# The down projection of a hybrid encoder block as seven part products over 2x2 blocks, in one stream with up

## The chip, the cores and the metric

The kernel runs on one core of a Trainium2 chip. The metric is the device time of one execution in microseconds, the median of several runs. A core has TensorE (PE in the profile: matmuls; PEld: its weight loads), VectorE (DVE), ScalarE (ACT), GpSimd (POOL) and SyncE (SP, which here issues all DMAs). All operands lie in SBUF, products in PSUM, which has eight banks of 128 partitions x 512 f32.

## What is computed

One layer of an encoder over x of 2048 tokens x 1024 channels, in f32: an input projection, an mLSTM head group and a latent attention group side by side, an output projection, a gated MLP with a centred convolution of three taps, and a gated per-layer embedding. What matters here is the MLP and what follows it:

```python
def conv_gated_mlp(xn, w_up, conv_w, conv_b, w_down):
    u = dwconv3_centred(xn @ w_up, conv_w, conv_b)
    gate, val = jnp.split(u, 2, axis=-1)
    return (jax.nn.silu(gate) * val) @ w_down
...
h = h + conv_gated_mlp(rms_norm(h, ln_ffn_g[l]), w_up[l], conv_ffn_w[l], conv_ffn_b[l], w_down[l])
gate = jax.nn.sigmoid(rms_norm(h, ple_norm_g[l]) @ w_ple_gate[l])
h = h + gate * rms_norm(p[l] @ w_ple_proj[l], ple_post_g[l])
return rms_norm(h, final_g)
```

w_up is 1024 x 5632 (gate and value halves of 2816), w_down is 2816 x 1024: 22 channel tiles of 128 on the side that down sums over.

## The kernel before

**Arithmetic.** Each f32 operand is split into a high part (rounded to the matmul's f32 format, by ACT) and a low part (the difference, by DVE): `split`, L112 to L119. A product of two split operands is three matmuls (`mm3`, L127: low x high, high x low, high x high), which accumulate into one PSUM bank. A matmul here has a stationary operand of 128 x 128 and a moving one of 128 x 512.

**Order.** The code is written with tile pools. A tile is taken by its tag (`at`, L103; tags x.., w.., t.., u..), and a tag is a place in SBUF: a new tile of a tag waits for the last reader of the old one. The scheduler of the framework orders the instructions of each engine's queue and each DMA when the kernel is built. It goes mainly by the order in which they are written, but takes later ones first where an earlier one would wait; at run time each queue is strictly in order. PSUM is four tiles of two banks (`two`, L167), from two pools by turns.

**Up (`up`, L1288).** 44 pairs: two passes over the tokens (tokens 0 to 1023, then 1024 to 2047), each over 22 channel tiles c. One pair computes the gate and the value columns of channel tile c for the pass's 1024 tokens. As a 2x2 by 2x2 block product it has the stationary blocks A11, A12 (gate columns, lower and upper half of the 1024 input channels) and A21, A22 (value columns), and the moving blocks B11, B12, B21, B22 (input channel halves x token halves of 512). Instead of eight block products, seven are made, with sums of blocks: A11·B11, S1·T1, S2·T2, A12·B21, S3·T3, A22·T4, S4·B22. Each is four channel tiles x three matmuls (`prod`, L1297). The seven need three banks x, y, z in which products of several outputs accumulate one after another, with evictions in between: x holds A11·B11 and then A12·B21 too, y holds S2·T2, then S3·T3, then A22·T4 too, z holds S1·T1 and later S4·B22 too. The last two products of a pair (`rest`, L1308) stand inside the next pair. A matmul that adds to a bank waits until the eviction that reads it is done: S3 waits for the add at L1385 that reads S2 out of y. x goes out through ACT (L1363, L1395), the rest through DVE.

The moving operands of a pass, split, lie in the x places (`OPX`, seven names). They are loaded from DRAM by `load_op` (L1207) through raw buffers t0 to t5, 28 pieces of 128 x 512 for a pass; T1 to T4 were formed by `sums` (L1174) and stored in `t_d`, for the second pass during pairs 6, 9, 12 and 15 of the first. At the last pair of the first pass, each name is replaced as soon as its last product is written (`last`, L1366 to L1410); T4 and B22 follow in the next pair.

The stationary operands of pair i+1 are split and summed by `up_prep` (L1256) within pair i, and the raw weights of pair i+2 are fetched by `up_load` (L1221). In the first pass the sums S are formed and kept in `s_d`; the second pass loads them.

`conv` (L1315) takes the finished gate and value columns of the previous pair, applies the three taps, SiLU and the product, and writes the hidden tile to `hid_d` in DRAM. It uses the places w7 and w11, and u0, u1, u2 for its inputs. After the last pair a short computation forms the hidden value of the last token (L1417 to L1425).

**Down (`down`, L1441).** Four blocks of 512 tokens. For each, eight PSUM banks (`facc`: four token tiles x 1024 output columns) accumulate over all 22 channel tiles: per channel tile, 4 token tiles x 2 halves x 3 matmuls. The hidden tile is the stationary operand (loaded and split once per block by `load_hid`, L1446), the rows of w_down are the moving one (loaded and split again in every block by `load_w`, L1432). At the end of a block the residual (`h1_d`) is added to `facc` (L1489) and the result is stored in `h2_d`.

**The last stage (`ple`, L1495)** is a generator. It is started at down's last block and advanced there at channel tiles 11 to 20 (L1476), which loads and splits the two tiles of w_ple_proj and the eight of w_ple_gate under the block's matmuls. The rest runs after down, over 16 token tiles: normalise, transpose, project, gate, final norm.

Of the kernel before, what the change touches and what calls it, by code (L numbers as in the profile page):

```python
# [19 lines left out]
P = 128  # L20
S = 2048
# [39 lines left out]
class Block:  # L61
# [4 lines left out]
    def __init__(self, ctx, tc, d):  # L66
# [30 lines left out]
        self.t_d = dt([2, 4, P, 4, 512], F32, name="t_d")  # L97
        self.s_d = dt([NC2, 2, P, D], F32, name="s_d")
# [47 lines left out]
    def run(self, out):  # L146
# [15 lines left out]
        self.up()  # L162
        self.down(out)
# [1006 lines left out]

    OPX = {"B11": (8, 9), "T1": (12, 13), "T2": (14, 15), "B21": (0, 1), "T3": (2, 3), "T4": (4, 5), "B22": (6, 7)}
    PAIRS = (("w3", "w4"), ("x10",), ("w5", "w6"), ("x11",), ("w8", "w9"))

    def sums(self, b):  # L1174


        nc = self.nc
        t0 = b * 2 * SB
        if not b:
            self.xop = {n: self.op_places(n) for n in ("B11", "T1", "T2")}  # L1180
        for k in range(4):
            r = []
            for i in range(4):
                kt, o = k + i // 2 * 4, t0 + i % 2 * SB
                r.append(self.at(f"t{i}", [P, SB], name="tsum"))
                nc.sync.dma_start(r[i], self.x2_d[:, kt, o:o + SB])
            b11, b12, b21, b22 = r
            tt = nc.vector.tensor_tensor
            put = lambda n, t: self.split(t, self.xop[n][0][:, k], self.xop[n][1][:, k])
            if not b:  # L1190
                put("B11", b11)
            tt(b12, b12, b11, op=ALU.subtract)
            tt(b22, b22, b12, op=ALU.subtract)
            tt(b11, b22, b11, op=ALU.subtract)
            tt(b21, b21, b22, op=ALU.subtract)
            if not b:
                put("T1", b12)
                put("T2", b22)
            for i, t in enumerate((b12, b22, b11, b21)):
                if b or i > 1:  # L1200
                    nc.sync.dma_start(self.t_d[b, i, :, k], t)
            yield

    def op_places(self, n):
        return [self.at(f"x{x}", [P, 4, SB], F32R, f"op{e}") for x, e in zip(self.OPX[n], "hl")]

    def load_op(self, b, n):  # L1207

        hi, lo = self.xop[n] = self.op_places(n)
        for k in range(4):  # L1210
            raw = self.at(next(self.orot), [P, SB], name="opr")
            if n[0] == "T":
                src = self.t_d[b, int(n[1]) - 1, :, k]
            else:
                o = b * 2 * SB + (int(n[2]) - 1) * SB
                src = self.x2_d[:, (int(n[1]) - 1) * 4 + k, o:o + SB]
            self.nc.sync.dma_start(raw, src)
            self.split(raw, hi[:, k], lo[:, k])
            yield

    def up_load(self, i):  # L1221


        nc = self.nc
        b, c = divmod(i, NC2)
# [18 lines left out]

    def up_pair(self, src):
        self.npair = getattr(self, "npair", -1) + 1
        tags = self.PAIRS[self.npair % 5]
        if len(tags) == 1:
            t = self.at(tags[0], [P, 2, D], F32R, "fw2")
            hi, lo = t[:, 0], t[:, 1]  # L1250
        else:
            hi, lo = [self.at(t, [P, D], F32R, "fw1") for t in tags]
        self.split(src, hi, lo)
        return [(hi[:, o:o + SB], lo[:, o:o + SB]) for o in (0, SB)]

    def up_prep(self, i):  # L1256

        nc = self.nc
        b, c = divmod(i, NC2)
# [5 lines left out]
        a22 = flat(raw[1]) if b else flat(raw[1])[:, SB:]  # L1265
        d = self.at(("w2", "w10")[i % 2], [P, 2, SB], F32R, "fwd")
# [4 lines left out]
        else:  # L1271
            sv, sg = flat(raw[1]), g
            lo, hi = slice(0, SB), slice(SB, D)
# [3 lines left out]
        ops["S3"], ops["S1"] = self.up_pair(sv)  # L1277
        if not b:
            nc.sync.dma_start(self.s_d[c, 0], sv)
# [353 lines left out]
```

## Time and profile before

| | us |
|---|---|
| median of three runs (lowest, highest) | 3025.64 (3020.70, 3027.59) |
| the profiled execution's own time | 3022.41 |
| its span, first to last instruction | 3020.6 |
| up: 1438 to 2280 in that span | 842 |
| down: 2280 to 2780 | 500 |
| last stage: 2780 to the end | 240 |

The granted clock of the profiled execution is 0.997 of full speed, on its one core.

How to read a profile's rows here: a group has the line, engine, operation, the tile written and the tiles read, the shape and the count, then the total busy time and the mean of one in ns, then the idle time of that engine ahead of these instructions with what ended it. A window row has a stretch of the span and each engine's busy time within it. A timeline row has the start and the length, both in us. A wait row has who waited for whom, and then the total, the times and the longest. Since the split and the matmul are helpers, L119, L116 and L129 stand for many places; the names of tiles tell them apart: `facc` is down, `fxy` and `fzs` are up's banks (x with y, z with a spare), `fw`, `fws` and `fwd` are weights, `oph` and `opl` moving operands.

### The profile page before, as it was taken

How to read it: one execution, taken by the hardware profiler on the slowest of the kernel's cores; microseconds unless marked ns; L12 is line 12 of the kernel's file. 1: busy time of each engine (PE TensorE's matmuls, PEld its weight loads, DVE VectorE, ACT ScalarE, POOL GpSimd, SP SyncE). 2: the span in 40 equal slices, each digit the busy share in tenths (PEclk: the TensorE clock that was granted, in tenths of full speed). 3: DMA queues.
4: the chain of work that ended last, by engine and by line, in shares of the span. 5: the costliest groups of instructions: out<-in, count | busy, mean ns of one | idle time of the engine just before them, and what ended most of it. 6: DMA issues, size and time to landing. Idle time of an engine off the chain costs nothing. (4 is left out here: it accounts for less than half of the span.)

```text
span 3020.6 us, 40579 instructions
## 1 busy us (share of the span) xinstructions
PE 2966.4 (98%) x15122; PEld 2505.6 (83%) x15122; DVE 1892.7 (63%) x3441; ACT 1355.2 (45%) x2598; POOL 141.5 (5%) x262
## 2 busy tenths in 40 slices
PE   8999999999999999999999999999999999999998
PEld 7888887889888888888778877888887888878887
DVE  7421556767767777646888889777776333334665
ACT  7211545556565566423444446444445232223444
POOL 3100000000000000001000000000000000000111
PEclk9999999999999999999999999999999999999999
DMA  6522445343323333668654445334337465444221
GB/s 191 110 76 91 139 126 167 111 138 118 95 93 97 95 125 114 192 209 268 229 188 139 140 139 197 126 124 126 126 122 251 167 209 202 133 153 148 79 79 63
DMA packets 322917, 430.03 MB, mean 142 GB/s; under 512 B 24976, under 2 KB 218528, under 8 KB 322720
## 3 DMA queue, kind: packets, MB, share of 16 engines
q1 hardware_dynamic: 322720, 427.44, 44.0%
q8 instruction: 119, 1.95, 0.3%
q14 instruction: 78, 0.64, 0.1%
HBM read 292.17 MB, written 135.20 MB: 141 GB/s over the span
## 5 line engine op out<-in xcount | busy, mean ns | idle before, releaser
L129 PE MATMUL facc<-fw,hid 128*128 128x512 f32 x2112 | 482.0, 390 | 6.2 <-DVE ug L1313 2.7
L129 PEld LDWEIGHTS facc<-fw,hid 128*128 128x128 f32 x2112 | 397.2, 188 | 90.1 <-DVE ug L1313 3.1
L129 PE MATMUL fxy<-oph,fw 128*128 128x512 f32 x1408 | 449.5, 392 | 6.0 <-DVE ug L1385 5.0
L129 PEld LDWEIGHTS fxy<-oph,fw 128*128 128x128 f32 x1408 | 264.2, 188 | 75.1 <-DVE ug L1385 11.5
L119 DVE TENSOR_TENSOR fw<-fwr,fw 128x1024 fp32r<-128x1024 f32 x176 | 215.1, 1223 | 163.0 <-ACT fw L116 162.9
L116 ACT CAST fw<-fwr 128x1024 fp32r<-128x1024 f32 x176 | 184.9, 1051 | 258.7 <-PE facc L129 123.2
L129 PE MATMUL fxy<-opl,fw 128*128 128x512 f32 x704 | 274.8, 390 | 0.0
L129 PE MATMUL bk<-wsp,xh 128*128 128x512 f32 (+1 forms) x768 | 234.4, 386 | 1.5 <-DVE wsp L125 1.4
L129 PE MATMUL fzs<-oph,fw 128*128 128x512 f32 x704 | 234.3, 389 | 1.2 <-DVE xt L1134 1.2
L116 ACT CAST pt<-tb 128x512 fp32r<-128x512 f32 x256 | 146.8, 586 | 192.8 <-PE tb L959 192.5
L129 PE MATMUL ppv<-pt,kv 128*128 128x256 f32 x1536 | 203.3, 287 | 0.0
L901 DVE TENSOR_REDUCE mx<-bk 128x1 f32<-128x512 f32 x256 | 174.7, 684 | 44.9 <-PE bk L900 43.6
L119 DVE TENSOR_TENSOR pt<-tb,pt 128x512 fp32r<-128x512 f32 x256 | 173.9, 685 | 35.8 <-ACT pt L116 34.1
L129 PEld LDWEIGHTS ppv<-pt,kv 128*128 128x128 f32 x1536 | 188.8, 191 | 0.0
L919 ACT ACTIVATE pe<-bk,nm 128x512 f32<-128x512 f32 x256 | 174.2, 694 | 25.5 <-DVE nm L913 24.4
L129 PE MATMUL pgp<-pw,x3s 128*128 128x512 f32 (+1 forms) x792 | 178.7, 385 | 0.0
L129 PE MATMUL bk<-wo,yhl 128*128 128x512 f32 x744 | 175.4, 392 | 0.0
L129 PEld LDWEIGHTS pgp<-pw,x3s 128*128 128x128 f32 x792 | 144.4, 188 | 28.3
L129 PEld LDWEIGHTS bk<-wsp,xh 128*128 128x128 f32 x768 | 144.2, 189 | 28.3 <-DVE wsp L125 3.5
L129 PEld LDWEIGHTS bk<-wo,yhl 128*128 128x128 f32 x744 | 138.2, 188 | 28.1
L129 PE MATMUL bk<-wsp,xl 128*128 128x512 f32 (+1 forms) x384 | 150.5, 392 | 9.6 <-ACT wsp L124 8.5
L129 PE MATMUL bk<-xh,wqk 128*128 128x512 f32 x480 | 156.8, 393 | 0.0
(322 smaller groups left out, 5352.4 us busy)
## 6 DMA issues: line engine op xcount, KB each, us to landing
fwr<-in_w_down SPq DMA_DIRECT2D x88, 512.0 KB, 3.8
fwr<-in_w_up SPq DMA_DIRECT2D x66, 512.0 KB, 4.1
s_d<-fwr SPq DMA_DIRECT2D x44, 512.0 KB, 3.2
fws<-s_d SPq DMA_DIRECT2D x44, 512.0 KB, 3.6
hraw<-hid_d SPq DMA_DIRECT2D x33, 512.0 KB, 4.2
rw<-row_d SPq DMA_DIRECT2D x32, 512.0 KB, 4.9
hid_d<-fgv SPq DMA_DIRECT2D x22, 512.0 KB, 3.5
hid_d<-fgv SPq DMA_DIRECT2D x22, 511.5 KB, 5.1
```

The source lines that it names most:

```text
L116: nc.scalar.copy(hi, src)
L119: (sub or nc.vector).tensor_tensor(lo, src, _f(hi), op=ALU.subtract)
L129: mm = lambda *a, **k: self.nc.tensor.matmul(*a, **k, skip_group_check=more)
L901: nc.vector.tensor_reduce(s.mx[:, kb:kb + 1], ps, axis=AX.X, op=ALU.max)
L919: nc.scalar.activation(s.pe[:, kb % 2], s.banks[kb], AF.Exp, bias=s.nm, scale=ASCALE, accum_out=s.rs[:, kb:kb + 1])
```

## The change

`up` and `down` become one method, `up_down`, with one list of five blocks of pairs: the two passes of up as before, and three parts of down. A part of down covers 8, 8 and 6 of the 22 channel tiles that down sums over. Each part has eight pairs, one for every two token tiles. In a down pair the stationary blocks are hidden rows (token tile x half of the part's channel tiles) and the moving blocks are parts of w_down (half of the channel tiles x 512 output columns): two halves of 4, 4 or 3 channel tiles. The seven products run as in up, with 12 matmuls each (9 in the third part).

The two output tiles of a pair are loaded into `fh` tiles (`down_out`: `h1_d` in the first part, `h2_d` after it), every product's bank is added into them by DVE, and they are stored to `h2_d`: outputs go through DRAM three times. The five places for them (`hrot`) are u0, w7, w11, u1, u2. For the first down pair the load stands behind the last `conv`; from then on it stands one pair ahead.

The stationary operands come from `down_load` (two tiles of 128 tokens from `hid_d`) and `up_prep`, which forms the sums as in the first pass of up but keeps none. The moving sums T1 to T4 of w_down are formed by `wsums` and kept in `tw_d`: the first part's during four pairs of up's second pass, the others' during the part before. `load_op` replaces the operands at the last pair of each block, as it did between the passes. The x places are cut anew: a place holds two channel tiles, each with its high and low part, and in the third part neighbouring names share places, so that x1, x5 and x13 become free.

```diff
-        self.up()
-        self.down(out)
+        self.up_down(out)
...
+    OPX3 = {"B11": (8, 8, 9), "T1": (9, 12, 12), "T2": (14, 14, 15), "B21": (15, 0, 0), "T3": (2, 2, 3), "T4": (3, 4, 4),
+            "B22": (6, 6, 7)}
+    NUP = 2 * NC2
+    BLOCKS = ((0, NC2, 4), (NC2, NC2, 4), (2 * NC2, 8, 4), (2 * NC2 + 8, 8, 4), (2 * NC2 + 16, 8, 3))
...
+    def wsums(self, g):
+        kk = self.BLOCKS[2 + g][2]
+        for k in range(kk):
+            self.sum4(lambda i: self.w_down(g, k, i), lambda i: self.tw_d[g, i, :, k], {})
+            yield
...
+    def sum4(self, src, dst, ops):
...
+        for i in range(4):
+            r.append(self.at(f"t{i}", [P, SB], name="tsum"))
+            nc.sync.dma_start(r[i], src(i))
+        b11, b12, b21, b22 = r
...
+        tt(b12, b12, b11, op=ALU.subtract)
+        tt(b22, b22, b12, op=ALU.subtract)
+        tt(b11, b22, b11, op=ALU.subtract)
+        tt(b21, b21, b22, op=ALU.subtract)
...
+        for i, t in enumerate((b12, b22, b11, b21)):
+            if not ops or i > 1:
+                nc.sync.dma_start(dst(i), t)
...
+    def down_load(self, i):
+        nc = self.nc
+        g, pr = divmod(i - self.NUP, 8)
+        n = 2 * self.BLOCKS[2 + g][2]
+        tags = ("w12", "w13", "w0", "w1")[i % 2 * 2:i % 2 * 2 + 2]
...
+            nc.sync.dma_start(t[:, :, :m], self.hid_d[8 * g:8 * g + n, :, o:o + m].rearrange("c p t -> p c t"))
...
+    def down_out(self, i):
+        g, pr = divmod(i - self.NUP, 8)
+        out = []
+        for e in range(2):
+            t = self.at(next(self.hrot), [P, D], name="fh")
+            self.nc.sync.dma_start(t, (self.h2_d if g else self.h1_d)[2 * pr + e])
+            out.append(t)
+        return out
...
         def rest(s):
             prod(s.y, s.ops["A22"], "T4", True)
-            tt(s.uv[:, 2:2 + SB], s.p1, s.y, op=ALU.add)
+            if s.down:
+                add(s.o[1][:, L], s.o[1][:, L], s.y)
+                nc.sync.dma_start(self.h2_d[2 * s.pr + 1], s.o[1])
+            else:
+                add(s.uv[:, 2:2 + SB], s.p1, s.y)
             prod(s.z, s.ops["S4"], "B22", True)
...
+                add(s.o[0][:, H], s.o[0][:, H], s.z)
+                nc.sync.dma_start(self.h2_d[2 * s.pr], s.o[0])
...
+        self.hrot = _rot("", ("u0", "w7", "w11", "u1", "u2"))
...
             prod(x, s.ops["A11"], "B11")
...
+            if s.down and s.o:
+                add(s.o[0][:, H], s.o[0][:, H], x)
+                o2 = s.o[1].rearrange("p (a t) -> p a t", a=2)
+                add(o2, o2, x.unsqueeze(1).broadcast_to([P, 2, SB]))
...
             if prev:
                 rest(prev)
+                if prev.i == NUP - 1:
+                    conv(prev)
+                    s.o = self.down_out(i)
+                    add(s.o[0][:, H], s.o[0][:, H], x)
...
             prod(s.y, s.ops["S2"], "T2")
+            if s.down:
+                add(s.o[0][:, H], s.o[0][:, H], s.y)
...
             prod(x, s.ops["A12"], "B21", True)
+            if s.down:
+                add(s.o[0][:, L], s.o[0][:, L], x)
...
+            if s.down and i + 1 < n:
+                outs[i + 1] = self.down_out(i + 1)
...
             prod(s.y, s.ops["S3"], "T3", True)
+            if s.down:
+                add(s.o[1][:, H], s.o[1][:, H], s.y)
+                add(s.o[1][:, H], s.o[1][:, H], s.z)
```

`ple` is advanced within the last part (`side`): the two projection weights, the first gate weight and the norm gain at its pairs 2, 3 and 4, the loading and the norm of token tile 0 at pair 5, the transposes of that tile into the spare bank of z at pairs 6 and 7, gate weights 1 to 6 within pair 7 as each of the operands' places comes free, and gate weight 7 and the first projection ahead of the last `rest`. The gain is applied in two halves, since it now lies in t4 and t5. Its other tiles have other places; the loop over the token tiles stays.

## The prediction

> **What bounds the kernel now.** I read the page's busy times first, then windows of the two stages that change, then the rows of the pair of products that the change reuses.
>
> ```profile
> span 3020.6 us, 40579 instructions
> ...
> PE 2966.4 (98%) x15122; PEld 2505.6 (83%) x15122; DVE 1892.7 (63%) x3441; ACT 1355.2 (45%) x2598; POOL 141.5 (5%) x262
> ...
> 1438.00:2280.00 842.00, 833.28 (x3648) 1.00 0.46 151
> 2280.00:2780.00 500.00, 493.79 (x2172) 1.00 0.54 182
> 2780.00:3020.00 240.00, 232.94 (x1104) 0.99 0.22 76
> ...
> L129 PE MATMUL facc<-fw,hid 128*128 128x512 f32 x2112 | 482.0, 390 | 6.2 <-DVE ug L1313 2.7
> ...
> 2523.64 36.66 PE L129 MATMUL facc<-fw,hid 128*128 128x512 f32 x161
> ```
>
> The last three columns of a window are granted clock, DMA share, GB/s. PE is idle for 8.7 us of up (1438 to 2280), 6.2 of down (2280 to 2780) and 7.1 of the last stage: everywhere the number of matmuls sets the time. Matmuls overlap, so the 390 ns of one is not its price; 161 of them in a row take 36.66 us, of which the last shows 0.39, so one costs 36.27 / 160 = 0.2267 us. Down's 2112 are 478.8 us.
>
> Up is already made of seven part products, so its pairs show what a down pair will look like.
>
> ```profile
> 2243.10 0.68 DVE L1385 TENSOR_TENSOR ug<-p,fxy 128x512 f32<-128x512 f32 x1
> ...
> 2262.17 0.68 DVE L1385 TENSOR_TENSOR ug<-p,fxy 128x512 f32<-128x512 f32 x1
> ...
> 1460.00:1850.00 390.00, 385.22 (x1680) 1.00 0.47 158
> ...
> 1489.00:1508.00 19.00, 18.37 (x81) 14.77 (x80) 17.38 (x24) 8.47 (x11) 0.00 (x0) 1.00 0.73 247
> 1603.00:1622.00 19.00, 19.00 (x85) 15.43 (x84) 15.57 (x21) 8.47 (x11) 0.00 (x0) 1.00 0.40 139
> 1850.00:1869.00 19.00, 18.71 (x82) 15.03 (x81) 17.93 (x26) 14.70 (x24) 0.00 (x0) 1.00 0.92 290
> 1869.00:1888.00 19.00, 18.08 (x78) 14.18 (x77) 18.59 (x26) 13.21 (x22) 0.00 (x0) 1.00 0.71 235
> 1888.00:1907.00 19.00, 17.82 (x79) 14.27 (x78) 16.61 (x25) 8.14 (x11) 0.00 (x0) 1.00 0.40 134
> 1926.00:1945.00 19.00, 19.00 (x85) 15.67 (x84) 13.73 (x16) 8.46 (x11) 0.00 (x0) 1.00 0.37 124
> ```
>
> One pair of up is 84 matmuls and lasts 19.07 us. After the window's length the columns are PE, PEld, DVE, ACT, POOL busy, then clock and DMA. The first of these 19 us windows is a first-pass pair that also runs a step of `sums` (DVE 17.4), the second a plain first-pass pair (15.6), the next three the change of pass, the last a plain second-pass pair (13.7). PE loses nothing in plain pairs; it loses when DVE is near full.
>
> **What is removed.** Down needs 7 products x (4+4+3) channel tiles x 3 matmuls x 8 token pairs = 1848 matmuls instead of 2112: 264 fewer, at 0.2267 us a gain of **59.8 us**, all on PE, the bounding engine. The old down's own idle, **6.2 us**, goes too. The two waits behind most of it (facc behind L1313, and behind weight splits) are re-priced below.
>
> **What a down pair adds to DVE and ACT.**
>
> ```profile
> L119 DVE TENSOR_TENSOR fw<-fwr,fw 128x1024 fp32r<-128x1024 f32 x176 | 215.1, 1223 | 163.0 <-ACT fw L116 162.9
> L119 DVE TENSOR_TENSOR fwd<-fwr,fwd 128x512 fp32r<-128x512 f32 x44 | 30.4, 692 | 0.1
> L1275 DVE TENSOR_TENSOR fwr<-fwr 128x512 f32<-128x512 f32 x22 | 15.2, 691 | 0.7
> L1489 DVE TENSOR_TENSOR fh<-fh,facc 128x1024 f32<-128x1024 f32 x16 | 19.0, 1218 | 7.3 <-PE facc L129 6.5
> L119 DVE TENSOR_TENSOR opl<-opr,oph 128x512 fp32r<-128x512 f32 x44 | 28.4, 686 | 3.6 <-ACT oph L116 2.8 <-PE bk L129 0.7
> ```
>
> `up_prep` of a down pair is three 1024-wide splits, one of 512 and four sums: 3 x 1.223 + 0.692 + 4 x 0.691 = 7.1 us. The outputs are seven 512-wide adds (0.69, as the sums) and the broadcast add of x into both halves (1024 wide, 1.218 as L1489): 6.0 us. Together 13.1 us beside 19.04 us of PE. In the third part 512 wide costs 0.69 and 1024 wide 1.22, so 768 is 0.96 and 384 is 0.56: 5.7 + 6.0 = 11.7 us beside 63 matmuls, 14.28 us. That is 69% and 82% of the pair; 13.73 and 15.57 of 19 (72% and 82%) ran without loss above. ACT does 3.8 us of casts and stays far from bounding. Steady cost: the rows run from nothing (the 1926 window) to (390 - 385.22) = 4.8 us over 20.5 pairs, 0.23 each, with steps of `sums` and none. I take the latter, since `wsums` runs in seven of the 24 pairs and weight splits of the last stage in others: 24 x 0.23 = **5.6**, bounds 0 and 18. The upper bound comes from this wait:
>
> ```profile
> who waited for it (us, times):
>   PEld fxy L129: 11.5, 22
>   PE fxy L129: 5.0, 6
> ```
>
> These are the matmuls that waited for the eviction at L1385, that is for S3 to go into the bank that S2 left. The two rows partly count the same gaps; added, they are 16.5 / 22 = 0.75 us where it happened, and x, which ACT evicts in up (L1363, L1395), is then DVE's too: 24 x 0.75 = 18.
>
> The first `wsums` puts four steps of 4 x 0.69 = 2.7 us into second-pass pairs: 13.7 + 2.7 = 16.4 of 19, less than the 17.4 above, which lost 0.63. I take **1 us**, bounds 0 and 2.5.
>
> **The change from up to down (pairs 43 and 44)** is the dear place. Twenty operand splits of 0.686 (13.7 us) land in pair 43, eight (5.5) in 44, as at the change of pass. There DVE's work is 15.6 + 13.7 + 13.7 + 5.5 = 48.5 us, less the 5.5 of T4 and B22, which have another pair's time: 43.0 over two pairs of 19.07, 4.9 too much, and the three windows lost 0.29 + 0.92 + 1.18 = 2.4 us. Here pair 43 has 13.7 + (7.1 - 4.4 of a second-pass prep) + 13.7 = 30.1, and pair 44 has 13.1, plus the last `conv`, which without a next pair's conv to hide among comes on top:
>
> ```profile
> 2295.28 0.39 PE L129 MATMUL fzs<-oph,fw 128*128 128x512 f32 x1
> ...
> 2303.31 0.19 DVE L1420 TENSOR_TENSOR elast<-edge,fcw 128x44 f32<-128x44 f32 x1
> 2303.43 1.28 DVE L1327 SCALAR_TENSOR_TENSOR fgv<-ug,fcw,fgv 128x1024 f32<-128x1024 f32 x1
> ...
> 2306.00 1.23 DVE L1333 TENSOR_TENSOR fgv<-fgv 128x1024 f32<-128x1024 f32 x1
> ...
> fh<-h_d SPq DMA_DIRECT2D x16, 512.0 KB, 6.0
> ```
>
> 4 x 1.28 + 1.23 + five short edge terms like L1420's, 1.0, is 7.4: 26.0 with its 5.5 of splits, 20.5 without; 50.6 over 38.1, 12.5 too much. By the ratio of the pass change the first half of its 4.9 is absorbed, so 12.5 - 2.5 = **10 us** is lost. A second way agrees roughly. Pair 44's outputs are loaded only behind that conv (`down_out(44)` needs w7, the buffer of the last conv), so x cannot leave its bank until then: last product of pair 43 to the end of L1333 took 11.6 us here (2295.67 to 2307.23), the load 6.0, the adds 0.7 + 1.2: 19.5 us in which PE has S2 and S3 of 44 and A11, S1, S2 of 45, five products of 12 x 0.2267 = 13.6 us: 6 short. PE does take such work from ahead of the program's order (facc matmuls stand among the last up pair's). On SP, behind the waiting load, stand pair 46's hidden rows and the loads of T4 and B22; on DVE, behind x's add, y's and the splits of 45. Bounds: 2.4, and 19.5 if nothing fills it.
>
> **The changes between the parts (51/52, 59/60)** have no conv: DVE 13.1 + 13.7 + 13.1 = 39.9 over 38.1, below the pass change. DMA is what could bind. A pair moves 2 x 512 KB each of hidden rows, old outputs and new outputs (3.1 MB), and the operands 28 x 256 KB (7.3 MB): 13.6 MB in 38 us. The best 19 us row is 290 GB/s, at which this takes 47 us, 9 too long. SP's issues are no bound:
>
> ```profile
> L1217 SPq DMA_DIRECT2D opr<-t_d x24: 319/323/994, 1371.2 to 1871.8; - x24
> ```
>
> 6 in a plain pair and 20 more at a change are 26 x 0.32 = 8.3 of 19 us. T4 and B22 may slip a pair, and the 139 GB/s of plain pairs leaves room. I take 3 each, **6 us**, bounds 1 and 18 for both. The Trainium skill ("DMA: Bandwidth & Descriptors", Specifications) gives 435 GB/s as the fabric's ceiling. By that rule the 13.6 MB take 31 us and these 6 us vanish (2975); the row at share 0.92 stays a third below it, so I keep the row.
>
> **The end.** Gate weights 1 to 7 move from the old block 3 into the last pair and behind it.
>
> ```profile
> pwr<-in_w_ple_gate SPq DMA_DIRECT2D x8, 512.0 KB, 4.3
> ...
> L116 ACT CAST pw<-pwr x10: 1048/1052/1055, 2710.3 to 2770.3; 128x1024 fp32r<-128x1024 f32 x10
> L119 DVE TENSOR_TENSOR pw<-pwr,pw x10: 1218/1225/1227, 2711.5 to 2771.6; 128x1024 fp32r<-128x1024 f32 x10
> ```
>
> Two raw buffers turn round in 4.3 + 1.05 + 1.22 = 6.6 us, 3.3 a weight. Two are there when S1 of the last pair frees their places, some 4 us into it; the seventh is split 1.2 + 2.5 x 6.6 later, near 22 to 23 us. PE has the pair (14.3), `rest` (4.1), the first projection (2.7) and the gate's products with the first seven weights (21 x 0.2267 = 4.8): 26 us of cover. I take **2**, bounds 0 and 8 (if that cover is gone, one turn of a buffer and more). The transposes and projection of token tile 0 only move; the last stage is otherwise the same.
>
> **The sum.** The profiled execution took 3022.41 us, 1.8 more than its span of 3020.6; the median of the runs shown is 3025.64, 3.2 above it, so against that the same saving would read 2984. 3022.4 - 59.8 - 6.2 + 5.6 + 1 + 10 + 6 + 2 = **2981.0 us**.
>
> The longest wait of PE in these stages is
>
> ```profile
> PEld facc L129 <- DVE ug L1313: 3.1, 1, 3.1
> ```
>
> and the granted clock stays at 1.00 in every window of them. The Trainium skill ("TensorE: Matmul & The Clock Gate", Part 1) says that PE falls to half its clock after an idle window of about 3.4 us, which speaks against a stall such as the one at pair 44. By that rule the matmuls of one such window take twice as long, an estimate of 2 to 3 us more (2984); no row here shows it.
>
> **Rivals.** (a) All cover works: only the pass-change price at 43/44 and the steady idle remain: 3022.4 - 66.0 + 2.4 + 5.6 = 2964. For it: no loss in 1603 to 1622 at DVE 82%. Against it: each of three changes brings more than the pass change did. Chance 0.14. (b) DMA binds at the part changes and in the four pairs with `wsums` (3.1 + 2.1 MB in 19 us, 275 GB/s): 18 instead of 6 at the changes and 1 in each of those pairs: 2997. For it: share 0.92 at 1850; against it: the operands can be fetched early. Chance 0.12. (c) Slower: the y bank becomes a round trip. In each down pair S3 waits for DVE to evict S2, and the next pair's `rest` for it to evict S3, with DVE deep in `up_prep`; in the third part only 2.04 us of A12 lie between. The longest single waits were
>
> ```profile
> PE fxy L129 <- DVE ug L1385: 5.0, 6, 1.7
> ...
> PEld fxy L129 <- DVE ug L1385: 11.5, 22, 2.1
> PEld fxy L129 <- DVE uv L1404: 1.9, 2, 1.6
> ```
>
> (total, times, longest). If every pair paid both, 2.1 + 1.6 = 3.7, it is 24 x 3.7 = 88.8: 3022.4 - 66.0 + 88.8 + 19 = 3064. It decides from (66.0 - 19) / 24 = 1.96 us a pair, four times today's mean wait. DVE then would be at some 80% of the stage, and it ran at 94% (17.93 of 19) with almost no loss; hence 0.12. (d) That there is no saving in matmuls can't be: the loop counts give 1848. The forecast has the remaining 0.62, with a range of its own from 2968 (no steady idle, the pass-change price at 43/44) to 2993 (0.75 us in every pair).
>
> **How the numbers follow.** Some 6 us, 0.2%, is about what a measurement tells from no change. Forecast, (a) and (b) are all faster, 0.88; I move 0.04 of it to "same", for several terms at their upper ends together. Faster 0.84, same 0.04, slower 0.12. The range 2960 to 3008 leaves out most of (c) and a little at the bottom.
>
> **What would show it.** Right: 264 matmuls fewer; the down pairs 19.0 us apart in two parts and 14.3 in the third; about 10 us of PE idle around the last conv, behind DVE adds into `fh`; DVE over 85% busy in down. Wrong: idle of PE above 1 us in plain down pairs, or clock below 1.00 there; idle at the part changes with the DMA share below 0.9 (then not DMA); a hole of more than 8 us before the first gate products.

## The result, and the profile after

| | before | after |
|---|---|---|
| median, us (lowest, highest, runs) | 3023.73 (3020.70, 3027.59, 4) | 2995.83 (2990.93, 2999.29, 4) |
| ratio, 95% interval | | 0.9906 (0.9887 to 0.9925) |
| profiled execution, span | 3020.6 | 2989.1 |

The kernel became 28 us faster by the medians and 31.5 by the two profiled spans; 2981.0 was forecast, 41.4 below the profiled execution of before. So the direction holds, and of the forecast 41 us 10 are missing by the spans and 13.5 by the medians. From up's first product to the last stage's first gate product it took 1344.8 us before (1438.69 to 2783.44) and takes 1315.4 after (1435.90 to 2751.33), 29.3 less; the rest of the 31.5 lies almost all ahead of up, where nothing was changed. The page of after, its span, busy times and traffic:

```profile
span 2989.1 us, 40727 instructions
...
PE 2917.3 (98%) x14858; PEld 2452.2 (82%) x14858; DVE 2072.1 (69%) x3798; ACT 1350.2 (45%) x2644; POOL 141.5 (5%) x262
...
HBM read 294.53 MB, written 163.51 MB: 153 GB/s over the span
```

264 matmuls fewer, as counted, and DVE's share up from 63 to 69%. Where the missing time lies is read from the windows of after (length, then PE, PEld, DVE, ACT, POOL busy with counts, granted clock, DMA share, GB/s):

```profile
1888.00:2260.00 372.00, 370.27 (x1626) 304.09 (x1625) 276.13 (x329) 164.79 (x214) 0.00 (x0) 1.00 0.47 147
...
2279.00:2298.00 19.00, 17.26 (x76) 13.74 (x75) 18.97 (x27) 14.37 (x24) 0.00 (x0) 1.00 0.76 241
2298.00:2317.00 19.00, 3.73 (x10) 2.23 (x8) 15.90 (x25) 7.59 (x11) 0.00 (x0) 0.57 0.64 206
2317.00:2336.00 19.00, 16.75 (x71) 13.02 (x71) 15.01 (x21) 2.74 (x3) 0.00 (x0) 0.99 0.78 261
2336.00:2450.00 114.00, 113.23 (x494) 91.50 (x493) 80.38 (x109) 26.32 (x31) 0.00 (x0) 1.00 0.66 223
2450.00:2510.00 60.00, 56.43 (x244) 45.17 (x243) 52.17 (x77) 22.95 (x33) 0.00 (x0) 1.00 0.90 299
2510.00:2610.00 100.00, 100.00 (x438) 81.24 (x437) 72.21 (x97) 21.97 (x26) 0.00 (x0) 1.00 0.61 207
2610.00:2660.00 50.00, 50.00 (x219) 40.38 (x218) 46.69 (x74) 22.22 (x36) 0.00 (x0) 1.00 0.85 285
2660.00:2735.00 75.00, 73.21 (x319) 57.96 (x318) 56.41 (x84) 18.05 (x24) 0.73 (x2) 1.00 0.53 188
2735.00:2775.00 40.00, 38.66 (x175) 30.88 (x174) 26.27 (x37) 18.89 (x31) 4.22 (x10) 1.00 0.58 201
```

PE's idle in order: the second pass (1.7 us of PE idle), the change from up to down (1.74 + 15.27 + 2.25 = 19.3 idle), the first part (0.8), the change to the second (3.6), the second (0), the change to the third (0), the third (1.8), the end (1.3). All but one are small; one window of 19 us holds ten matmuls. This is its timeline (start, length, engine, line, tile written and read, and in brackets the idle time ahead with what ended it; in after L130 is the matmul, L120 the low part of a split, L1363 every add, L1411 the convolution's product, L1308 the load of an output block):

```profile
2295.62 2.88 PE L130 MATMUL fzs<-op,fw 128*128 128x512 f32 x12
...
2308.86 1.22 DVE L1411 TENSOR_TENSOR fgv<-fgv 128x1024 f32<-128x1024 f32 x1
...
2310.09 2.49 DVE L120 TENSOR_TENSOR op<-opr,op 128x512 fp32r<-128x512 f32 x4
...
2310.52 0.38 SPq L1308 DMA_DIRECT2D fh<-h_d  x1
...
2312.49 1.22 DVE L120 TENSOR_TENSOR fw<-hraw,fw 128x1024 fp32r<-128x1024 f32 x1
...
2313.77 3.35 PE L130 MATMUL fxy<-op,fw 128*128 128x512 f32 x7 [15.27 <-DVE fw L120]
...
2316.49 1.22 DVE L1363 TENSOR_TENSOR fh<-fh,fxy 128x1024 f32<-128x1024 f32 x1 [0.72 <-DMA fh<-h_d]
...
2317.77 0.50 PE L130 MATMUL fxy<-op,fw 128*128 128x512 f32 x1 [0.65 <-DVE fh L1363]
```

The last product of pair 43 (S4·B22) ends at 2298.5. PE then waits for the low part of pair 45's first weights, which stands in DVE's queue behind the last convolution and the operand splits. Behind the first seven matmuls of pair 45's A11·B11, in PE's queue as it was planned, stand pair 44's S2·T2, A12·B21 and S3·T3, and S2·T2 starts when x has been added into the output block: the block is loaded into w7, which comes free with the convolution's product at 2310.08; the load is issued at 2310.52 and x is added by 2317.7.

Plain pairs of down are near what was forecast. Two successive starts of the same product run, in the first part and in the third:

```profile
2396.53 11.26 PE L130 MATMUL fxy<-op,fw 128*128 128x512 f32 x48
...
2415.79 4.47 PE L130 MATMUL fxy<-op,fw 128*128 128x512 f32 x19
...
2675.49 8.57 PE L130 MATMUL fxy<-op,fw 128*128 128x512 f32 x36
...
2690.01 8.54 PE L130 MATMUL fxy<-op,fw 128*128 128x512 f32 x36
```

19.26 and 14.52 us a pair, against 19.04 and 14.28 by count. These 0.2 us do not show as idle: a matmul's row is 390 ns long and the next starts after 227, so a wait under 0.16 us vanishes in the overlap.

### The profile page after: what moved, and what is told of

Read it like the earlier page. It is cut to its first block, busy times and chain, and to the rows that moved or that the text cites. A ratio compares the mean times of both kernels' runs of the same rounds, so it can differ in the third digit from the quotient of the medians.

```text
span 2989.1 us, 40727 instructions
## 1 busy us (share of the span) xinstructions
PE 2917.3 (98%) x14858; PEld 2452.2 (82%) x14858; DVE 2072.1 (69%) x3798; ACT 1350.2 (45%) x2644; POOL 141.5 (5%) x262
## 5 line engine op out<-in xcount | busy, mean ns | idle before, releaser
L130 PE MATMUL fxy<-op,fw 128*128 128x512 f32 x3168 | 751.3, 393 | 28.7 <-DVE fw L120 16.7
L130 PEld LDWEIGHTS fxy<-op,fw 128*128 128x128 f32 x3168 | 587.4, 188 | 176.2 <-DVE fh L1363 17.8
L130 PE MATMUL fzs<-op,fw 128*128 128x512 f32 x1584 | 385.9, 389 | 0.9 <-DVE xt L1134 0.9
L130 PEld LDWEIGHTS fzs<-op,fw 128*128 128x128 f32 x1584 | 297.1, 188 | 63.0 <-DVE xt L1134 1.1
L130 PE MATMUL bk<-wsp,xh 128*128 128x512 f32 (+1 forms) x768 | 234.9, 387 | 1.2 <-DVE wsp L126 1.0
L130 PE MATMUL ppv<-pt,kv 128*128 128x256 f32 x1536 | 203.3, 287 | 0.0
L120 DVE TENSOR_TENSOR pt<-tb,pt 128x512 fp32r<-128x512 f32 x256 | 174.1, 686 | 35.6 <-ACT pt L117 33.9
L130 PE MATMUL fxy<-op,fwd 128*128 128x512 f32 x792 | 191.8, 391 | 6.4 <-DVE fh L1363 3.4
L130 PEld LDWEIGHTS ppv<-pt,kv 128*128 128x128 f32 x1536 | 188.8, 191 | 0.0
L130 PEld LDWEIGHTS fxy<-op,fwd 128*128 128x128 f32 x792 | 148.0, 188 | 39.9 <-DVE fh L1363 4.9
L130 PE MATMUL pgp<-pw,x3s 128*128 128x512 f32 (+1 forms) x792 | 178.9, 385 | 0.6 <-DVE pw L120 0.6
L130 PE MATMUL bk<-wo,yhl 128*128 128x512 f32 x744 | 175.4, 392 | 0.0
L130 PEld LDWEIGHTS pgp<-pw,x3s 128*128 128x128 f32 x792 | 144.4, 188 | 29.4 <-DVE pw L120 1.1
L130 PEld LDWEIGHTS bk<-wsp,xh 128*128 128x128 f32 x768 | 144.5, 189 | 28.4 <-DVE wsp L126 3.2
L1363 DVE TENSOR_TENSOR fh<-fh,fxy 128x512 f32<-128x512 f32 (+1 forms) x144 | 109.6, 773 | 75.3 <-PE fxy L130 72.8
L130 PEld LDWEIGHTS bk<-wo,yhl 128*128 128x128 f32 x744 | 138.2, 188 | 28.1
L130 PE MATMUL bk<-wsp,xl 128*128 128x512 f32 (+1 forms) x384 | 150.8, 393 | 9.1 <-ACT wsp L125 9.0
L117 ACT CAST fw<-hraw 128x1024 fp32r<-128x1024 f32 (+1 forms) x72 | 70.5, 982 | 192.1 <-PE fxy L130 124.0
L130 PE MATMUL bk<-xh,wqk 128*128 128x512 f32 x480 | 156.8, 392 | 0.0
```

Source lines behind the costliest of these rows:

```text
L117: nc.scalar.copy(hi, src)
L120: (sub or nc.vector).tensor_tensor(lo, src, _f(hi), op=ALU.subtract)
L130: mm = lambda *a, **k: self.nc.tensor.matmul(*a, **k, skip_group_check=more)
L1363: add = lambda o, a, b: tt(o, a, b, op=ALU.add)
```

## The experiments

All are edits of the kernel after. The window 2279 to 2360 is their first yardstick, since whole times are too coarse: the passes of up ahead of it, which most edits leave alone, differ by more from one profiled execution to the next than an edit is worth (after, then the third experiment):

```profile
1440.00:2260.00 820.00, 811.00 (x3545) 660.22 (x3546) 655.32 (x818) 374.72 (x496) 0.00 (x0) 1.00 0.49 162
```
```profile
1440.00:2260.00 820.00, 803.76 (x3498) 653.22 (x3497) 649.57 (x812) 371.88 (x498) 0.74 (x2) 1.00 0.49 160
```

9.0 us of idle in one, 16.2 in the other, in stages that are written alike. Why is open; after's profiled execution was the fastest of its four. The results together, where idle is 81 us less PE's busy time from 2279 to 2360, and matmuls those in it. This window stands at a fixed time, while up's last product ends between 2298.5 (after) and 2312.6 us (9), so it holds another piece of the work in each kernel. The last column does not depend on that, and it counts slow matmuls too: the time from the start of pair 41's A22·T4 to that of pair 49's (in after 2252.52 to 2429.59), 672 matmuls, 152.3 us by count. Each value is of one profiled execution; how far this stretch differs between executions of one kernel was not measured.

| kernel | time, us (runs) | idle | matmuls | longest wait of PE | stretch, us |
|---|---|---|---|---|---|
| after | 2995.83 (4) | 19.3 | 259 | 15.3 | 177.1 |
| 1 x copied out | 2999.45 (2) | 15.0 | 269 | 11.7 | 175.2 |
| 2 weights first | 2996.88 (2) | 15.8 | 258 | 9.0 | 176.3 |
| 3 both | 2999.76 (4) | 11.9 | 270 | 4.7 | 177.0 |
| 4 no last taps | 2990.95 (1) | 13.0 | 284 | 9.6 | 170.8 |
| 5 no low parts | 2993.65 (1) | 12.6 | 277 | 6.4 | 175.6 |
| 6 low parts on GpSimd | 3000.40 (2) | 17.9 | 241 | 11.4 | 182.3 |
| 7 low parts stored | 3003.51 (4) | 11.4 | 283 | 6.7 | 176.1 |
| 8 sums early | 2999.29 (4) | 16.8 | 268 | 14.8 | 174.0 |
| 9 sums early, no low parts | 3000.09 (1) | 13.7 | 275 | 7.4 | 172.3 |
| 10 output places | 2993.04 (4) | 14.6 | 268 | 5.9 | 175.4 |
| 11 written order | 3003.86 (2) | 25.9 | 222 | 18.6 | 184.7 |
| 12 free places | 2991.69 (4) | 11.9 | 288 | 3.1 | 169.9 |

**1 to 3: which of the two waits.** The first theories were that DVE's queue order holds pair 45's split (D), or that the output load behind the convolution holds x (X). In 1, ACT copies pair 44's x out of its bank, as in up, so x need not wait for the output block:

```diff
-            if s.down:
+            if s.down and i > NUP:
                 s.o = outs.pop(i) if i in outs else None
             else:
+                s.o = None
                 s.p1 = self.at(f"t{6 + i % 2}", [P, SB], name="p1")
                 nc.scalar.copy(s.p1, x)
```

> Pair 44 copies x out of its bank with ScalarE as an up pair does, so A12 no longer waits for the output tiles that are loaded behind the last conv. Theory D (the hole of 15.3 us is VectorE's queue: the split of pair 45's first operand stands behind the last conv and eight operand splits): PE gains A12 and perhaps S3 of pair 44 as filling, 2.7 to 5.4 us, and still waits 10 us or more. Theory X (the hole is the output load behind the conv): the hole goes to 5 us or less, and the time falls by 12 us or more against the changed kernel (2995.8).

In 2, pair 45's weights are prepared ahead of pair 43's rest and the convolution; 3 has both edits:

```diff
+            if i == NUP:
+                self.up_prep(i + 1)
             if prev:
                 rest(prev)
...
-            if i + 1 < n:
+            if i + 1 < n and i != NUP:
                 self.up_prep(i + 1)
```

> The operand splits of pair 45 are written ahead of the last conv, nothing else moves. Theory D: A11, S1 and S2 of pair 45 fill up to 8.2 us of the hole, PE waits 7 to 9 us in all around it, time some 8 us below the changed kernel. Theory X: x stays in its bank until its adds, which now come later by what went ahead of them; the idle time only moves behind the fill, 12 us or more in sum, gain under 5 us.

> Both edits. If both waits stand side by side (each hides the other), neither alone closes the hole and both together do: under 4 us of PE idle there, granted clock 1.00 in that stretch, 15 to 18 us below the changed kernel, near 2979. If DMA or ScalarE holds the stretch, 8 us or more stay.

PE's timeline in 2:

```profile
2310.44 4.62 PE L130 MATMUL fzs<-op,fw 128*128 128x512 f32 x12 [3.44 <-DVE fw L120]
2324.08 4.97 PE L130 MATMUL fxy<-op,fw 128*128 128x512 f32 x12 [9.03 <-DVE fh L1363]
```

The wait for the split shrinks and one for the add into the output block takes its place, 15.8 us in all, as X had it for this edit. In 1, though x itself has been copied away, 11.7 us stay, as D had it; they end with the add of y, which DVE does at 2318.27, behind the convolution. In 3 there are three waits of 2.7 to 4.7 us, where under 4 in all was expected. The edits take 3.4 to 7.3 us of idle and lose most of it to slow matmuls (the granted clock falls around such waits, see the last section): the stretch is only 0.1 to 1.9 us shorter. Neither wait alone is the cause, and the two together are not all of it either.

**4: the last convolution without its taps.** Left out are four multiply-adds, 5.1 us of DVE, in the convolution of pair 43.

```diff
-                for tap in (1, 2):
+                for tap in (1, 2) if s.i != NUP - 1 else ():
```

> The last pair's conv leaves out its four tap sums (5.1 us of VectorE). Theory D and theory X both have the conv in their chain: the hole shrinks by about 5 us, to 10. If the hole is DMA (operand pieces landing late), it stays near 15.

Idle fell by 6.3 us, the stretch by 6.3 too: the stall follows the convolution's length nearly one for one. That fits a sum of DVE work (W) and a chain through the convolution alike.

**5: the same through DVE's work alone.** The operands' low parts are left out, 18.3 us of DVE, none of it in the convolution.

```diff
-            self.split(raw, hi, lo)
+            if blk == 2:
+                self.nc.scalar.copy(hi, raw)
+                ops[k] = hi, hi
+            else:
+                self.split(raw, hi, lo)
```

> The 28 low-part subtractions of the first down part's inner operands (18.3 us of VectorE between 2260 and 2345 us) are left out, the high part standing in for the low one in the products, so that the output is not the reference's. TensorE, transfers and ScalarE do what they did. Theory W (VectorE's work in pairs 43 to 45 is longer than TensorE's time for them, and the stall is the excess): leaving out 5.1 us took 5.7 us off, so leaving out over 18 us takes the whole stall away: idle of TensorE between 2279 and 2336 us under 3 us instead of 19.3, up to first gate product 1297 to 1301 us instead of 1315.4, time 2978 to 2983. Rival T (the operands and output halves arrive late by transfer, VectorE is only the last in the chain): at least 8 us of idle stay in the same place, 1307 us or more.

Over three times the work of 4 came out, yet idle fell hardly further, to 12.6, and the stretch by 1.5 us only, where 4 brought 6.3. By the prediction's sum DVE now has time enough (50.6 less 13.7 for the splits of pair 43, beside 38.1), so work alone is not the cause and W fell in this form. Who ended waits in 5 from 2285 to 2345 (total, times, longest; L1367 is here the add):

```profile
PEld fxy L130 <- DVE fh L1367: 8.5, 5, 4.6
DVE fh L1367 <- DMA fh<-h_d: 7.0, 3, 3.5
...
PE fzs L130 <- DVE fw L120: 6.4, 1, 6.4
```

DVE itself now waits 7 us for output blocks. The chain from pair 43's last product, which ends at 2302.7, to the end of the add of x has kept its length, 18.4 us against 19.2 in after:

```profile
2319.91 1.22 DVE L1367 TENSOR_TENSOR fh<-fh,fxy 128x1024 f32<-128x1024 f32 x1 [3.54 <-DMA fh<-h_d]
```

**6 and 7: the low parts made elsewhere.** Of the 28 subtractions, the 16 of T operands go to GpSimd (6), or are made in the second pass and stored (7):

```diff
-            self.split(raw, hi, lo)
+            self.split(raw, hi, lo, sub=self.nc.gpsimd if blk == 2 and n[0] == "T" else None)
```
```diff
+            if blk == 2 and n[0] == "T":
+                self.nc.scalar.copy(hi, raw)
+            else:
+                self.split(raw, hi, lo)
+        if blk == 2 and n[0] == "T":
+            for k, (hi, lo) in enumerate(ops):
+                self.nc.sync.dma_start(_f(lo), self.lo_d[int(n[1]) - 1, :, k])
```

> The 16 low-part subtractions of the first down part's T operands go to GpSimd, which does nothing in this stretch; the 12 others stay. VectorE gives up 11 us. Theory W: if a subtraction takes GpSimd 0.8 to 1.5 us (its nearest row on 512 columns, the mask's select, takes 0.817), the stall falls from 19 to about 8 us and the time to about 2985; if it takes over 2 us, four of them stand ahead of a product of 2.7 us and the stall moves to them, time 2990 to 3010. Rival T: no change of more than 2 us, 2994 to 2998.

> The low parts of the same 16 T operands are made in the second pass of up (four a pair, in pairs 29, 32, 35 and 38, from sums read back), stored, and loaded straight into their places at the change of passes; the output is the reference's. VectorE's work is moved, not removed: 11 us less in pairs 43 to 45, 2.8 us more in each of four pairs that have some 3 us to spare; 4.2 MB more of loads at the change, 8.4 MB more in the second pass. Theory W: the stall falls from 19 to 8 us or less, up to first gate product 1304 to 1307 us, time 2984 to 2989. Rival T: more loads at the change make it worse, 2996 to 3005.

Groups of instructions in 6 from 2255 to 2345 us, GpSimd's and then two of DVE's (busy, mean ns of one):

```profile
L120 POOL TENSOR_TENSOR op<-opr,op 128x512 fp32r<-128x512 f32 x16 | 25.6, 1628 | 846.9 <-ACT op L117 846.8
```
```profile
L120 DVE TENSOR_TENSOR fw<-hraw,fw 128x1024 fp32r<-128x1024 f32 x7 | 9.7, 1390 | 0.0
...
L1352 DVE TENSOR_TENSOR hraw<-hraw 128x512 f32<-128x512 f32 x2 | 2.5, 1235 | 0.0
```

A subtraction takes GpSimd 1.63 us instead of DVE's 0.69, and DVE's own operations are slower in this stretch: 1.39 us for 1.22, and two sums of 512 columns at a mean of 1.24 for 0.69. The 1.63 lies between the two cases of W (0.8 to 1.5, and over 2), idle fell by 1.4 us and the stretch is 5.3 us longer, so 6 decides nothing. In 7 the stall fell to 11.4, near 5's 12.6 but not to the 8 of W, and the stretch is 1.0 shorter. The DMA share from 2298 to 2317 rose from 0.64 to 0.99, and the second pass, which makes the low parts, lost 6.9 us (1888 to 2260) where after lost 1.7; the time is 7.7 us above that of after, in the range of T, but with 5.1 us more of idle in the second pass.

**8 and 9: the transfers too.** The weight sums of the second part move from pairs 46 to 49 into the second pass; 9 also leaves the low parts out.

```diff
-(NUP, (2, 3, 4, 5)), (NUP + 8, (2, 3, 4)))):
+(NC2, (7, 10, 13, 16)), (NUP + 8, (2, 3, 4)))):
```

> The weight sums of the second down part (the four steps in pairs 46 to 49, whose loads and adds came as early as 2313 us) are made in the second pass of up, in pairs 29, 32, 35 and 38; the output is the reference's. From 2260 to 2345 us that takes away up to 5.5 us of VectorE and some 5 of the 20.9 MB moved. Theory WT (two limits one behind the other at the change: VectorE's work first, and where it is cut, as in the run without the low parts, the loads of operands and of output halves, 0.87 of the DMA engines' time from 2298 to 2317): the idle of TensorE from 2279 to 2336 falls from 19.3 to about 13 us, up to first gate product 1308 to 1310 us, time 2988 to 2991. Rival O (the order in which the queues were planned makes the stall, neither amount matters): same loss within 3 us, 1312 to 1319 us, 2993 to 2999, or any value without relation to the amounts. The second pass pays 0 to 2 us for the 11 us of adds put into it.

> The same, and the 28 low-part subtractions of the first down part's inner operands left out as well (the high part stands in for the low one, so the output is not the reference's): both limits are eased, VectorE by some 24 us and the transfers by 5 MB. Theory WT: less than 5 us of idle left between 2279 and 2336 us, up to first gate product 1298 to 1302 us. Rival O: over 10 us of idle left, 1307 us or more.

Theory WT missed both times. In 8 the idle fell by 2.5 us only and the second pass paid 4.2 more; in 9, with some 24 us of DVE and 5 MB of traffic gone, 13.7 us stayed. O's marks came true in 9 (12.1 us idle to 2336, 1320.6 us to the first gate product) and in part in 8 (its idle, not its 1324.2). DVE's timeline in 9 shows one of the waits (L1367 the add):

```profile
2330.78 1.22 DVE L1367 TENSOR_TENSOR fh<-fh,fxy 128x1024 f32<-128x1024 f32 x1 [6.13 <-DMA fh<-h_d]
```

The add of x waits 6 us for the block whose place the convolution held; PE stands 4.7 us behind it, and 7.4 behind a weight split that DVE did in the midst of the convolution. Amounts explain only part of the stall; the place became the next suspect.

**10 to 12: the place and the order.** 10 gives pair 44's second output block the two p1 places, t6 and t7, and loads it and adds x ahead of the convolution. 11 keeps after's places and makes PE go through pairs 44 and 45 as written. 12 takes places that are free earlier (u0, t5, t6; t5 is no longer a raw buffer of the first part's operands), loads them in pair 43 and puts the last convolution where the others stand, behind A12·B21.

```diff
+            if i == self.NUP and e:
+                t = [self.at(f"t{6 + f}", [P, SB], name="fh2") for f in range(2)]
+                for f in range(2):
+                    self.nc.sync.dma_start(t[f], src[:, f * SB:f * SB + SB])
...
                 if prev.i == NUP - 1:
-                    conv(prev)
                     s.o = self.down_out(i)
-                    add(s.o[0][:, H], s.o[0][:, H], x)
...
+                    add_x(s, x)
+                    conv(prev)
```
```diff
+        with self.tc.manual_schedule(engines={mybir.EngineType.PE}):
+            pair(NUP)
+            pair(NUP + 1)
```
```diff
-                if prev.i == NUP - 1:
-                    conv(prev)
-                    s.o = self.down_out(i)
...
-            if s.down and i + 1 < n:
-                outs[i + 1] = self.down_out(i + 1)
-            if prev and not s.down:
+            if prev and not prev.down:
                 conv(prev)
+            if NUP - 1 <= i < n - 1:
+                outs[i + 1] = self.down_out(i + 1)
```

> Pair 44's second output block goes to the places of the two p1 tiles of up (free after the products of pair 43) instead of the place w7, which the last convolution holds until its product; the block is loaded, and x added into it, ahead of that convolution. VectorE's and the transfers' amounts stay as they are; the output is the reference's. It also changes what the scheduler plans: pair 44's T2 and B21 products now stand ahead of pair 45's first one in TensorE's queue, where they stood behind it. Theory H (pair 44 cannot give up its x and y banks until the last convolution gives up a place and the output block has come, 5 us later, and the queue was planned around that: pair 45's first product stands ahead of three of pair 44): the 15.3 us wait goes, idle of TensorE from 2279 to 2336 falls from 19.3 to under 8 us, up to first gate product 1301 to 1306 us instead of 1315.4, time 2982 to 2988. Rival W (VectorE's sum of work in pairs 43 to 45): the sum is the same, 12 us or more of idle stay, 1311 or more, 2992 to 2998.

> TensorE goes through pairs 44 and 45 in the order in which they are written (T2, B21 and T3 products of pair 44 ahead of pair 45's first); places, loads and all other work as in the kernel after. Theory H: the order alone does not help, since x is added into the output block only at 2316.5, after the last convolution: the wait for the split goes and one for the adds of fh takes its place, 10 to 16 us, up to first gate product 1311 to 1317 us. Rival O (only the planned order makes the stall, pair 44's three products could have run): idle under 8 us, 1302 to 1307 us. Rival W: as H here, 12 us or more.

> Pair 44's output blocks go to places that nothing of up holds by then (u0, t5, t6), are loaded in pair 43, and x is added right after its product; the last convolution stands where the others do, behind pair 44's fourth product (B21), so that the adds of x and y of pair 44 no longer stand behind it in VectorE's queue. Pair 45's output blocks come behind that convolution, and the scheduler planned pair 46's first product ahead of pair 45's T2 product. VectorE's and the transfers' amounts are those of after, and so is the output. Theory H (who stands behind the convolution): the waits of pair 44 go, 2 to 4 us of them are left, and 2 to 6 us come back in pair 45; idle of TensorE from 2279 to 2360 us is 10 us or less instead of the 19 to 20 of after, up to first gate product 1303 to 1309 us, time 2983 to 2989. Rival W (VectorE has 12.5 us more work in pairs 43 to 45 than TensorE has time for them): the stall only moves, 12.5 us or more is left in pairs 44 to 46, 1311 us or more, 2992 to 2997.

PE's timeline in 10, then in 11:

```profile
2305.59 5.45 PE L130 MATMUL fxy<-op,fw 128*128 128x512 f32 x12 [5.31 <-DVE fh L1369]
2316.91 10.40 PE L130 MATMUL fxy<-op,fw 128*128 128x512 f32 x36 [5.87 <-DVE fh L1369]
```
```profile
2322.12 4.90 PE L130 MATMUL fxy<-op,fw 128*128 128x512 f32 x12 [18.63 <-DVE fh L1363]
2328.16 3.02 PE L130 MATMUL fxy<-op,fw 128*128 128x512 f32 x12 [1.13 <-DVE fh L1363]
```

and what DVE did ahead of these two in 11, the add of x and the add of y:

```profile
2320.85 1.22 DVE L1363 TENSOR_TENSOR fh<-fh,fxy 128x1024 f32<-128x1024 f32 x1 [0.45 <-DMA fh<-h_d]
...
2327.42 0.68 DVE L1363 TENSOR_TENSOR fh<-fh,fxy 128x512 f32<-128x512 f32 x1
```

11 settles one thing: with pair 44's products first in the queue, S2·T2 still waits for the add of x, 18.6 us, even longer than H put it. It goes into bank y and x is another bank, but S2·T2 starts only when the adds that read x are done, at 2322.07; in the same way A12·B21, which goes into bank x, starts only behind the add of y, at 2328.10. The two banks are one tile (`xy`), which fits; the same with two tiles was not tried. So the planned order was not the cause (O fell: 25.9 us of idle where it had under 8); running ahead to pair 45 was even the better order, with a stretch of 177.1 against 184.7. 10 shows the same step twice: S2·T2 behind the last add of x, then A12·B21 behind the add of y at 2316.2, which stood in DVE's queue behind the convolution. The 15.3 us wait went as H said, but 12.9 us of idle stayed from 2279 to 2336, where H had under 8. The marks of rival W came true in 10: 12 us or more, 1317.0 us to the first gate product, a time of 2993.04. So the place alone is not the gate.

In 12 neither wait is left at that size; its windows:

```profile
2298.00:2336.00 38.00, 31.92 (x129) 24.60 (x127) 37.09 (x55) 15.73 (x23) 0.00 (x0) 0.96 0.73 232
...
2279.00:2360.00 81.00, 69.12 (x288) 53.84 (x287) 72.16 (x104) 33.20 (x49) 0.00 (x0) 0.98 0.75 238
```

11.9 us of idle remain, spread over waits of 0.4 to 3.1 us, with 29 matmuls more than in after. DVE is busy for 37.09 of 38 us: here its work is the bound. H's 10 or less and W's 12.5 or more both miss narrowly; the size is nearer to W's. The stretch is 7.2 us shorter than in after, the most of all twelve. From up's first product to the first gate product it took 1316.1 us, as long as in after, because the passes ahead of the change lost 14.1 us in this execution and 9.0 in that one. The median, 2991.69, has the ratio 0.9888 (0.9868 to 0.9909) to before. It is the lowest of the versions timed in four runs, but its interval overlaps that of after, so that it is faster is not shown.

**What follows.** Two limits lie over each other. One is a chain through the last convolution to the place w7, the output block's load and the adds. The other is DVE's work in pairs 43 to 45. The chain, from pair 43's last product to the end of the add of x, is 19.2 us in after, 18.4 in 5, 19.4 in 9 and 18.6 in 11, whatever work is taken from DVE elsewhere; 4, which takes 5.1 us out of the convolution itself, has 14.3. Easing the work alone (5, 9) leaves 12.6 and 13.7 us of idle and shortens the stretch by 1.5 and 4.8, easing the chain alone (12) leaves 11.9 and shortens it by 7.2. That both limits together make up the whole is not shown: 12 together with 5, which by this reading should leave little, was not tried.

## Why the prediction was right, and which step was mis-sized

**What is removed** came out by count: 264 matmuls, 59.8 us, and the old down's idle.

**Steady cost**, forecast 5.6: visible idle in plain stretches is 0.77 + 0 + 1.79 = 2.6 us, and 0.2 us a pair is hidden in the overlap, 24 x 0.2 = 4.8: together 7.4. The waits behind it are those named:

```profile
PE fxy L130 <- DVE fh L1363: 8.8, 9, 1.7
...
PEld fxy L130 <- DVE fh L1363: 22.8, 43, 2.1
```

**The first `wsums`**, forecast 1: the second pass lost 1.7 us in all.

**The change from up to down**, forecast 10, is the mis-sized term: 19.3 us of idle and some 1.6 of slow matmuls. By the stretch it is some 2 us more: 177.1 - 152.3 = 24.8, of which eight pairs' steady 0.2 are 1.8. The two raw sums, 12.5 and 19.5, were good; what was taken off them was not. The second way gave 19.5 us from the last product of pair 43 until x is added; in the trace it is 2298.5 to 2317.7, 19.2. It then set 13.6 us of products against it, S2 and S3 of pair 44 and three of pair 45. Of these sixty matmuls seven ran before x was added, and only at the end. S2 waits for the add of x (11 shows it) and S3 stands behind S2, and pair 45's first product waited for a split that stands behind the same convolution on DVE. The bound "19.5 if nothing fills it" was the case. The first way gave 12.5 us too much work for DVE, and 2.5 of it was taken off by the ratio of the pass change. With the chain eased 12 shows 11.9, close to the 12.5, so little of it seems to be absorbed.

**The changes between the parts**, forecast 6: 3.6 and 0. DMA had a share of 0.90 and 0.85 there and hardly bound: of the 3.6 us, 3.4 ended with adds of DVE into `fh`, none of which waited for a transfer in that stretch. So the term was near in size at the first change and had the wrong reason, and rival (b) is out. Nor was the best row's 290 GB/s a ceiling: 7 moved 336 from 2298 to 2317. **The end**, forecast 2: 1.3. Rival (c), a round trip in every pair, is excluded by pairs of 19.26 us. Rival (a) needed the cover that was missing. Of the marks set beforehand two were wrong besides. The 15.3 us around the last convolution ended with a weight split and not with an add into `fh`. And DVE is not over 85% busy in plain down pairs but 71% (80.38 of 114), near the 69% worked out for them.

The sum of the measured terms is 7.4 + 1.7 + 19.3 + 1.6 + 3.6 + 1.3 = 34.9; 66.0 - 34.9 = 31.1. That this meets the 31.5 of the two spans is in part luck, since after's execution reached up 2.8 us earlier with nothing changed ahead of it; from up to the first gate product 29.3 were saved, so 1.8 us of loss are not in the sum. The median of after lies 4.9 above its profiled execution, the rest of the distance to 2981.0.

## What to carry to other kernels

When work is said to cover a wait, ask of each covering instruction what it waits for itself: here every one hung on the same convolution, by a shared tile, by a place or by an in-order queue. At a change of stage add up two things apart, the busiest engine's work and the longest chain of place, load and add, and expect the larger one whole, as it came here; cutting one alone brought 1.5 to 7.2 us of some 21. Two banks that are filled and emptied in turn should be two tiles if the framework's waits go by tile; this was not tried here.

## What the runs showed of the hardware

In the hole the granted clock fell. In after's window 2298 to 2317 it is 0.57, and the first seven matmuls take 3.35 us, their starts 0.43 apart instead of 0.2267. The Trainium skill ("TensorE: Matmul & The Clock Gate", Part 1) says that PE falls to half clock after an idle window of about 3.4 us; for this hole the trace agrees. The cost was estimated at 2 to 3 us and was about 1.6 here (seven matmuls at full clock take 6 x 0.2267 + 0.39 = 1.75), and holes of 4 to 6 us cost more: in 3 and in 10 twelve matmuls behind such a hole took 5.49 and 5.45 us instead of 2.88. But the length of the hole alone does not decide it. In after a hole of 1.74 us left the clock whole; in 2 one of 1.80 did not (PE's timeline in after, then in 2, then a window of 2, where the clock is 0.50):

```profile
2292.73 3.06 PE L130 MATMUL fxy<-op,fwd 128*128 128x512 f32 x12 [1.74 <-DVE uv L1363]
```
```profile
2296.93 4.60 PE L130 MATMUL fxy<-op,fwd 128*128 128x512 f32 x12 [1.80 <-DVE uv L1363]
```
```profile
2297.60:2301.00 3.40, 3.40 (x10) 2.63 (x9) 3.40 (x6) 1.14 (x2) 0.00 (x0) 0.50 0.82 299
```

In 12 twelve matmuls behind a hole of 2.50 us took 4.60 us as well. So here the half clock came after holes shorter than the 3.4 us too.

GpSimd took 1.63 us for what takes DVE 0.69, and while it ran some of DVE's operations took nearly twice their time (1.24 us for 0.69). The Trainium skill ("GPSIMD Engine Reference", Specifications) says that its access to SBUF is shared with DVE and contended by DVE instructions with two inputs in SBUF, which these are; the trace agrees, though the two were not run by themselves.
